# Seven products instead of eight in 30 weight blocks of a float32 encoder layer on one core

## The chip, the cores and the metric

The kernel runs on one core of one Trainium2 chip. The metric is the device time of one execution in microseconds; the median of three runs is compared. One more execution was profiled, and all rows below are from it.

## The reference

One encoder layer over 256 tokens of width 2048, in float32:

```python
z = rmsnorm(x, mix_norm) @ w_in          # latents, conv inputs, memory queries, 3*2048 gates
y_mla  = mla_attention(...) @ w_o_mla    # 8 heads
y_conv = (cb * dwconv3(cc * cv)) @ w_out_conv
y_mem  = memory_attention(...) @ w_o_mem # 4 heads, 256 memory tokens
gates  = sigmoid(g + gate_bias)          # (256, 3, 2048)
x = x + (gates[0]*y_mla + gates[1]*y_conv + gates[2]*y_mem) @ w_o
u = dwconv3(rmsnorm(x, ffn_norm) @ w_up) # 2*5632 columns
a, b = split(u)
x = x + (silu(a) * b) @ w_down           # 5632 -> 2048
return rmsnorm(x, final_norm)
```

## The kernel before

Every float32 matrix product is made of float32r halves: a value is its rounded part `hi` plus the rest `lo`, and a product is hi·hi + hi·lo + lo·hi, three matmuls. Weights come from HBM in blocks of 1 MB (128 partitions x 2048 floats) into the pool `raws` (3 buffers), issued on SP's queue (`load`, L130). For each block ScalarE copies `raw` to `hi` (L144) and VectorE subtracts, `lo = raw - hi` (L145); `his` has 3 buffers, `los` 2. Tokens and other activations are kept as pairs side by side in one tile: 256 columns of hi, 256 of lo, in a pool `slots` of 54 tiles. PSUM has two pools, `mmps` (5 banks) and `atps` (3 banks).

The program is written in order, stage by stage, without loops on the chip; a scheduler orders the instructions of each engine by priority and hands out buffers, so an engine's queue can differ a little from the source's order. Within an engine the order is then fixed, and each instruction waits for what it needs.

Stages: latents of the tokens, whose `xs` hold x times the norm's gain but not the token's own factor `rsb` (1/rms); the keys of the memory tokens, during which `token_factor` (L341) gets `rs`, `rsb`, and `rs2b` = rsb squared; the values of the memory tokens (`values`, L385, blocks of 24 matmuls); attention heads, mixed with the short convolution (`gated_conv`, L582), which multiply by `rsb` or `rs2b` wherever a product of `xs` is used; the gates and branch projections (L699 to L717); the output projection; the up projection (`up`, L752, 2 groups of 22 chunks of 128 columns); after each group the down projection over that group's 22 chunks (L793 to L800); for the last 512 columns a version that keeps the last 10 pieces of weights and ends with the final norm.

The gates: for each of 4 column groups n and each of 3 branches, `project` (L657) forms the gate product of 16 token chunks (4 blocks) and then the branch's projection (8 chunks, 2 blocks). `project` takes 2 banks, one for each half of the tokens, and calls `multiply` (L671 to L676) for each chunk and half:

```python
nc.tensor.matmul(ps, xh, hi[:, s], start=first, stop=False)   # L674
nc.tensor.matmul(ps, xh, lo[:, s], start=False, stop=False)   # L675
nc.tensor.matmul(ps, xl, hi[:, s], start=False, stop=final)   # L676
```

The stationary operand is 128 tokens, the moving one 512 weight columns. A block of four chunks is thus 24 matmuls. The gate's bank is read by VectorE (L708: times rs, plus bias), sigmoid follows on ScalarE (L711), then L715 and L717 on VectorE multiply the branch and add. `turned` (L678) transposes the merged columns, 8 transposes and 4 splits for each n, called from inside the next projection (`flush`).

Of the kernel before, what the change touches and what calls it, by code (L numbers as in the profile page):

```python
# [19 lines left out]
P = 128  # L20
D = 2048
# [44 lines left out]
KEPT = 10  # L66
STEPS = "r - k0 v0 - q0 0 1 2 3 k1 v1 q1 4 5 - 6 - 7 -"
# [9 lines left out]
def tile_kernel(ctx: ExitStack, tc: tile.TileContext, a, out):  # L77
# [5 lines left out]
    los = ctx.enter_context(tc.tile_pool(name="los", bufs=2))  # L83
# [26 lines left out]
    x0 = slots.tile([P, 2 * T], F32, tag="raw", name="xr", bufs=4)  # L110
# [148 lines left out]
    class Tokens:  # L259
# [6 lines left out]
        def load(self, n):  # L266

            i = len(self.raw)
            t = self.raw[-1][0] if i % 2 else slots.tile([P, 2 * T], F32, tag="raw", name="xr", bufs=4)
# [71 lines left out]
    def token_factor():  # L341
# [11 lines left out]
        rs2b = const.tile([P, T], F32, name="rs2b")  # L353
        nc.vector.tensor_tensor(rs2b, rsb, rsb, op=ALU.mult)
        yield rs, rsb, rs2, rs2b
# [27 lines left out]
    rs, rsb, rs2, rs2b = next(own)  # L383
# [167 lines left out]
    for i in range(8):  # L551
        qx.append(scaled(total(mm(*wblock(), 0, xs)), rsb, f"qx{i}", XD**-0.5))
        if i == 0:
# [8 lines left out]
            nc.vector.tensor_tensor(half(kr, 0), ps[:, 0:T], rsb, op=ALU.mult)  # L562
# [19 lines left out]
    def gated_conv():  # L582
        for i in range(8):
# [6 lines left out]
            nc.vector.tensor_tensor(v, v, rs2b, op=ALU.mult)  # L590
# [3 lines left out]
            t = temp("t")  # L594
            nc.vector.tensor_tensor(t, total(mm(*wblock(), 0, xs)), rsb, op=ALU.mult)
            nc.vector.tensor_tensor(u, u, t, op=ALU.mult)
# [95 lines left out]
    mg = [slot(f"mg{i}", F32R) for i in range(KC)]  # L692
# [6 lines left out]
    for n in range(NW):  # L699
        ms_ = [slot(f"m{h}") for h in range(2)]  # L700
        for br, (w, src) in enumerate((("woa", oa), ("woc", yc), ("wom", om))):
            bias = wide("bias")
            nc.scalar.dma_start(bias, a["gb"][:, br * D + n * 512 : br * D + (n + 1) * 512])
            gp = project(a["wg"], br * NW + n, xs, flush)
            gs = []
            for h in range(2):
                g = ms_[h] if br == 0 else wide("g")
                nc.vector.scalar_tensor_tensor(  # L708
                    g, gp[h], rs[:, h : h + 1], bias, op0=ALU.mult, op1=ALU.add
                )  # L710
                nc.scalar.activation(g, g, AF.Sigmoid)  # L711
                gs.append(g)
            bp = project(a[w], n, src)
            for h in range(2):
                nc.vector.tensor_tensor(gs[h], bp[h], gs[h], op=ALU.mult)  # L715
                if br:
                    nc.vector.tensor_tensor(ms_[h], ms_[h], gs[h], op=ALU.add)  # L717
        pending.append(lambda ms_=ms_, n=n: turned(ms_, mg[4 * n : 4 * n + 4]))
# [31 lines left out]
    rfb = []  # L750

    def up(c):  # L752
# [25 lines left out]
        s = half(us, 0)  # L778
        nc.scalar.activation(s, half(vs, 0), AF.Silu)
        nc.vector.tensor_tensor(s, s, half(vs, 1), op=ALU.mult)  # L780
        f = slot(f"f{c}", F32R)
        split(f, s)
        return f
# [3 lines left out]
    for g in range(NG):  # L787
# [5 lines left out]
        for n in range(NW - last):  # L793
            ps = project(a["wdn"], g * NW + n, fs)
# [35 lines left out]
    src = a["wdn"][(NG - 1) * NW + n]  # L830
# [48 lines left out]

def _colmajor(v):  # L880

    return np.asarray(v).reshape(-1, P).T


def _layout(x, mem, positions, mix_norm, w_in, q_norm, w_uq, kv_norm, w_ukv, w_o_mla, conv_w,
# [11 lines left out]
    for i in range(8):  # L897
# [28 lines left out]
        "wg": _groups(w_in[0][:, o_g:]),  # L926
# [7 lines left out]
        "wdn": _groups(w_down[0], NG),  # L934
# [22 lines left out]
```

## Time and profile before

| | us |
|---|---|
| median of 3 runs (1629.28 to 1630.43) | 1630.28 |
| the profiled execution | 1630.0 |
| its span, first to last instruction | 1628.2 |
| TensorE busy with matmuls | 1612.4 |
| VectorE busy | 1061.1 |
| ScalarE busy | 797.7 |

The profiled execution is 0.28 below the median, and 1.8 of it lie outside the span. A matmul's duration in the rows includes its way through the array; what a stream of them costs is the distance between their starts. The granted clock is that of TensorE, as a share of its 2.4 GHz.

### The profile page before, as it was taken

To read this page: it belongs to the slowest core of one execution; us is meant where nothing else is said; L and a number is where in the kernel's file an instruction comes from. 1 tells how busy PE (TensorE), PEld (TensorE's weight loads), DVE (VectorE), ACT (ScalarE), POOL (GpSimd) and SP (SyncE) were. 2 spreads that over 40 slices of the span, in tenths; PEclk is the share of its full clock that TensorE was granted. 3 is DMA by queue.
4 is the path that set the end of the run, shared out by engine and by line. 5 is a ranking of instruction groups with operands and counts; after the bars stand their busy time and mean duration, and the time that the engine had idled before them with its cause. 6 is when DMAs were issued, how large, how long until landed. Compare 5 with 4: busy or idle time off the path is not lost.

```text
span 1628.2 us, 20547 instructions
## 1 busy us (share of the span) xinstructions
PE 1612.4 (99%) x8322; PEld 1382.8 (85%) x8322; DVE 1061.1 (65%) x1291; ACT 797.7 (49%) x955; POOL 12.6 (1%) x23
## 2 busy tenths in 40 slices
PE   9999999999999999999999999999999999999997
PEld 8888898888888888888788888888888888888886
DVE  6866779776455554555545877777445777777444
ACT  7754556554434343443444655555333555555433
POOL 0000000000000000000000000000000000000000
PEclk9999999999999999999999999999999999999999
DMA  8655445445565565656555455555555555555553
GB/s 314 227 219 191 161 164 197 155 169 181 184 210 194 196 212 185 215 201 205 189 207 194 181 183 196 190 183 193 179 205 197 183 196 191 183 193 197 204 194 116
DMA packets 52142, 314.77 MB, mean 193 GB/s; under 512 B 6096, under 2 KB 7504, under 8 KB 16592
## 3 DMA queue, kind: packets, MB, share of 16 engines
q1 hardware_dynamic: 47520, 306.73, 53.1%
q10 hardware_dynamic: 3888, 6.20, 1.2%
q8 instruction: 65, 1.06, 0.3%
q0 software_dynamic: 640, 0.52, 0.1%
q14 instruction: 29, 0.24, 0.0%
HBM read 310.16 MB, written 2.10 MB: 192 GB/s over the span
## 4 chain that ended last, share of the span: by engine, by line
PE 96%; DVE 1%; ACT 1%; DMA 1%; issue 1%; ACTq 0%; POOLq 0%; POOL 0%; DVEq 0%
PE ps L172 27%; PE ps L174 16%; PE ps L675 15%; PE ps L676 15%; PE ps L674 14%; PE ps L176 2%; PE ps L398 1%; PE ps L399 1%; PE ps L397 1%; PE pss L463 1%; PE ps L185 1%; DVE lo L145 1%; PE ps L189 0%; PE ps L685 0%; PE pst L487 0%
## 5 line engine op out<-in xcount | busy, mean ns | idle before, releaser
L145 DVE TENSOR_TENSOR lo<-raw,hi 128x2048 fp32r<-128x2048 f32 (+2 forms) x297 | 644.5, 2172 | 355.9 <-PE ps L675 190.3
L144 ACT ACTIVATE hi<-raw 128x2048 fp32r<-128x2048 f32 (+2 forms) x297 | 539.7, 1820 | 429.8 <-PE ps L676 388.7
L172 PE MATMUL ps<-h,hi 128*128 128x512 f32 x1845 | 447.0, 392 | 0.2 <-ACT kn L205 0.2
L172 PEld LDWEIGHTS ps<-h,hi 128*128 128x128 f32 x1845 | 344.7, 188 | 68.8 <-ACT kn L205 0.4
L174 PEld LDWEIGHTS ps<-h,lo 128*128 128x128 f32 x1968 | 252.8, 191 | 9.6 <-DVE lo L145 0.2
L174 PE MATMUL ps<-h,lo 128*128 128x256 f32 x1968 | 257.2, 283 | 0.0
L675 PE MATMUL ps<-lo,h 128*128 128x512 f32 x384 | 149.9, 390 | 0.0
L676 PE MATMUL ps<-hi,h 128*128 128x512 f32 x384 | 149.6, 390 | 0.0
L674 PE MATMUL ps<-hi,h 128*128 128x512 f32 x384 | 142.7, 390 | 0.0
L676 PE MATMUL ps<-hi,f 128*128 128x512 f32 x332 | 129.3, 389 | 0.0
L675 PE MATMUL ps<-lo,f 128*128 128x512 f32 x332 | 129.3, 389 | 0.0
L674 PE MATMUL ps<-hi,f 128*128 128x512 f32 x332 | 123.5, 389 | 0.0
L196 ACT ACTIVATE hl<-ps 128x256 f32<-128x256 f32 x149 | 57.0, 383 | 90.1 <-PE ps L176 77.8
L676 PEld LDWEIGHTS ps<-hi,h 128*128 128x128 f32 x384 | 72.1, 188 | 14.9
L674 PEld LDWEIGHTS ps<-hi,h 128*128 128x128 f32 x384 | 72.1, 188 | 14.8
L675 PEld LDWEIGHTS ps<-lo,h 128*128 128x128 f32 x384 | 72.1, 188 | 14.8
L571 ACT ACTIVATE v<-u,taps 128x256 f32<-128x256 f32 x88 | 44.8, 509 | 72.3 <-DVE u L776 72.3
L572 DVE SCALAR_TENSOR_TENSOR v<-u,taps,v 128x255 f32<-128x255 f32 x88 | 42.6, 484 | 48.8 <-ACT v L571 48.8
L675 PEld LDWEIGHTS ps<-lo,f 128*128 128x128 f32 x332 | 62.3, 188 | 13.0
L674 PEld LDWEIGHTS ps<-hi,f 128*128 128x128 f32 x332 | 62.4, 188 | 12.9
L676 PEld LDWEIGHTS ps<-hi,f 128*128 128x128 f32 x332 | 62.3, 188 | 12.8
L198 DVE TENSOR_TENSOR t<-ps,hl 128x256 f32<-128x256 f32 x149 | 62.1, 418 | 2.6 <-ACT hl L196 2.4
(263 smaller groups left out, 1714.0 us busy)
## 6 DMA issues: line engine op xcount, KB each, us to landing
raw<-in_wup SPq DMA_DIRECT2D x88, 1024.0 KB, 4.8
raw<-in_wg SPq DMA_DIRECT2D x48, 1024.0 KB, 4.8
raw<-in_wdn SPq DMA_DIRECT2D x40, 1024.0 KB, 4.8
raw<-in_win SPq DMA_DIRECT2D x35, 1024.0 KB, 4.8
raw<-in_wo SPq DMA_DIRECT2D x16, 1024.0 KB, 4.9
raw<-in_wmk SPq DMA_DIRECT2D x8, 1024.0 KB, 4.8
raw<-in_wmv SPq DMA_DIRECT2D x8, 1024.0 KB, 4.8
raw<-in_woa SPq DMA_DIRECT2D x8, 1024.0 KB, 5.0
```

The lines of the kernel that those rows point to most:

```text
L144: nc.scalar.activation(hi[:, s], raw[:, s], AF.Copy)
L145: nc.vector.tensor_tensor(lo[:, s], raw[:, s], f32(hi[:, s]), op=ALU.subtract)
L172: nc.tensor.matmul(ps, hi[:, ks[k]], xs[k], start=first and k == 0, stop=False)
L174: nc.tensor.matmul(ps[:, 0:T], lo[:, ks[k]], xs[k][:, 0:T], start=False, stop=False)
L176: nc.tensor.matmul(ps, hi[:, ks[k]], xs[k], start=False, stop=True)
L196: nc.scalar.activation(hl, ps[:, T:], AF.Copy)
L198: nc.vector.tensor_tensor(t, ps[:, 0:T], hl, op=ALU.add)
L571: nc.scalar.activation(dst, x, AF.Copy, scale=col(w, wn + wi))
L572: nc.vector.scalar_tensor_tensor(dst[:, 1:T], x[:, 0 : T - 1], col(w, wi), dst[:, 1:T], op0=ALU.mult, op1=ALU.add)
L674: nc.tensor.matmul(ps, xh, hi[:, s], start=first, stop=False)
L675: nc.tensor.matmul(ps, xh, lo[:, s], start=False, stop=False)
L676: nc.tensor.matmul(ps, xl, hi[:, s], start=False, stop=final)
```

## The change

Two chunks of input (a pair p, two token chunks x1 and x2 of 128 features) by two column groups of 512 and two halves of the tokens are a 2x2 by 2x2 product of submatrices. A plain block does its 8 products. A fast block does 7 (Winograd's form of Strassen's scheme): sums of the weight pieces are made in place in `raw` after the first pieces are split, and split again into a second pair of hi/lo buffers; sums of token pieces are made once and kept. Results stand in eight banks: q1, q6, q7, q5, q2 in `mmps` (in this order), q3, q4, d in `atps`. At the end VectorE combines them.

Fast blocks: pairs 1, 3, 5 of 8 in each of 6 gate products (18 blocks), pairs 1, 3, 5, 7 of 11 in three down products (12 blocks). The down projection's last 1024 columns of the second group stay as they were. The gates go branch by branch (2, 1, 0), two column groups at a time: one gate product of 8 pair blocks, then two projections of 2 blocks each. The tokens are normed early: the 8 pairs are loaded again (8 DMAs on SP's queue), multiplied by gain and `rsb` and split anew into `xs`, while the memory values are formed; the later multiplications by `rsb`, `rs2b` and `rs` fall away. `los` has 3 buffers instead of 2, paid by the 4 tiles that held raw tokens, which now share the pool of `wide`.

```diff
+GATES = (1, 3, 5)
+FAST = (1, 3, 5, 7)
-    los = ctx.enter_context(tc.tile_pool(name="los", bufs=2))
+    los = ctx.enter_context(tc.tile_pool(name="los", bufs=3))
-    x0 = slots.tile([P, 2 * T], F32, tag="raw", name="xr", bufs=4)
+    x0 = wide("xr")
...
+    def normed(p):
+        t = wide("xn")
+        nc.sync.dma_start(t, a["xT"][:, 2 * p * T : 2 * (p + 1) * T])
+        for j in range(2):
+            h = half(t, j)
+            nc.vector.scalar_tensor_tensor(
+                h, h, col("mix", 2 * p + j), rsb, op0=ALU.mult, op1=ALU.mult
+            )
+            split(xs[2 * p + j], h)
     for n in range(2):
+        for p in range(4 * n, 4 * n + 4):
+            normed(p)
         vx.append(values(a["wmv"], n, 4, ms, "vx"))
...
-            nc.vector.tensor_tensor(v, v, rs2b, op=ALU.mult)
...
+    def token_sums(t):
+        a11, a21, a12, a22 = (t[:, i * P : (i + 1) * P] for i in range(4))
+        w = wide("sums")
+        s1, s2, s3, s4 = (w[:, i * P : (i + 1) * P] for i in range(4))
+        nc.vector.tensor_tensor(s1, a21, a22, op=ALU.subtract)
+        nc.vector.tensor_tensor(s3, a21, a11, op=ALU.subtract)
+        nc.vector.tensor_tensor(s2, a11, s1, op=ALU.subtract)
+        nc.vector.tensor_tensor(s4, a12, s2, op=ALU.subtract)
+        sh, sl = slot("sh", F32R), slot("sl", F32R)
+        nc.scalar.activation(sh, w, AF.Copy)
+        nc.vector.tensor_tensor(sl, w, f32(sh), op=ALU.subtract)
+        return sh, sl
+    class Two:
+        def __init__(self, src, xs, sums):
...
+            self.q = {name: psum() for name in ("q1", "q6", "q7", "q5", "q2")}
+            self.q.update({name: psum(atps, "at") for name in ("q3", "q4", "d")})
+        def add(self, name, xh, xl, hi, lo, piece):
+            s = slice(piece * 512, (piece + 1) * 512)
+            for x, w in ((xh, hi), (xh, lo), (xl, hi)):
+                nc.tensor.matmul(self.q[name], x, w[:, s], ...)
+        def plain(self, p):
+            hi, lo = block(self.src[:, p * WB : (p + 1) * WB])
+            for j, x in enumerate(self.xs[2 * p : 2 * p + 2]):
+                for h in range(2):
+                    for g in range(2):
+                        piece = ((0, 1), (3, 2))[j][g]
+                        self.add((("q2", "q3"), ("q4", "d"))[h][g], *self.part(x, h), hi, lo, piece)
+        def fast(self, p):
+            raw = next(load(self.src[:, p * WB : (p + 1) * WB]))
...
+            hi, lo = two(slice(0, 512), slice(1024, 2048))
+            nc.vector.tensor_tensor(raw[:, 0:1024], raw[:, 0:1024], raw[:, 512:1536], op=ALU.add)
+            nc.vector.tensor_tensor(b[2], b[0], b[2], op=ALU.add)
+            nc.vector.tensor_tensor(b[3], b[2], b[3], op=ALU.add)
+            hi2, lo2 = two(slice(0, 1024), slice(1024, 2048))
...
+            self.add("q1", *self.part(x1, 0), hi, lo, 0)
+            self.add("q3", *sums(4), hi, lo, 2)
+            self.add("q2", *self.part(x2_, 0), hi, lo, 3)
+            self.add("q5", *sums(1), hi2, lo2, 0)
+            self.add("q7", *sums(3), hi2, lo2, 1)
+            self.add("q6", *sums(2), hi2, lo2, 2)
+            self.add("q4", *self.part(x2_, 1), hi2, lo2, 3)
...
+    def gated(q, g, b1, b2):
+        (g11, g12), (g21, g22) = g
+        nc.scalar.activation(g11, q["q1"], AF.Copy)
+        to(g22, q["q6"], g11, ALU.subtract)
+        to(g12, g22, b2)
+        to(g12, g12, q["q5"])
+        to(g21, b1, g22, ALU.subtract)
+        to(g21, g21, q["q7"], ALU.subtract)
+        to(g22, g12, q["q7"])
+        to(g11, g11, b1)
+        for x, name in ((g11, "q2"), (g12, "q3"), (g21, "q4"), (g22, "d")):
+            to(x, x, q[name])
+            nc.scalar.activation(x, x, AF.Sigmoid)
+    for br, w, src in ((2, "wom", om), (1, "woc", yc), (0, "woa", oa)):
+        for jp in range(2):
...
+            q = Two(a["wg"][br * 2 + jp], xs, hsums).run()
+            gated(q, g, *bias)
+            for i in range(2):
+                bp = project(a[w], 2 * jp + i, src, flush)
...
-        for n in range(NW - last):
-            ps = project(a["wdn"], g * NW + n, fs)
+        for n in range(0, 2 if last else NW, 2):
+            q = Two(a["wd2"][g * NW // 2 + n // 2], fs, sums).run()
+            added(q, [[x2[h][n + i] for i in range(2)] for h in range(2)])
...
+        for n in range(2, NW - 1 if last else 2):
+            ps = project(a["wdn"], n - 2, fs)
```

(`two` splits the named pieces of `raw` into a fresh hi and a fresh lo buffer, ScalarE and VectorE; `added` is for the down projection what `gated` is for the gates: one copy and 12 additions into the residual; `token_sums` runs for 3 pairs before the gates and for 8 pairs in the up projection.)

How VectorE's queue changes in the gates. Before, between two gate products (`lo` is a block's rest, `ps` a bank):

```order
L145 TENSOR_TENSOR lo_4389<-raw_4386,hi_4388 128x2048 [waits DVE_49,DMAHW1_49,PE_49,Activation_49]
L708 SCALAR_TENSOR_TENSOR g_4378<-ps_4256,xr_1119,bias_4254 128x512 [waits DMAHW2_49,PE_49]
L145 TENSOR_TENSOR lo_4419<-raw_4416,hi_4418 128x2048 [waits DVE_49,DMAHW2_49,PE_49,Activation_49]
L708 SCALAR_TENSOR_TENSOR g_4381<-ps_4257,xr_1119,bias_4254 128x512 [waits PE_49]
L145 TENSOR_TENSOR lo_4457<-raw_4454,hi_4456 128x2048 [waits DVE_49,DMAHW3_49,PE_49,Activation_49]
L715 TENSOR_TENSOR g_4378<-ps_4384,g_4378 128x512 [waits PE_49,Activation_49]
```

Now, a plain block (lo_4677), a fast block (first pair of buffers lo_4707, second lo_4716), a plain block, and the first reading of a bank:

```order
L147 TENSOR_TENSOR lo_4677<-raw_4674,hi_4676 128x2048 [waits DMAHW3_49,Activation_49]
L767 TENSOR_TENSOR lo_4707<-raw_4704,hi_4706 128x512 [waits DMAHW4_49,Activation_49]
L767 TENSOR_TENSOR lo_4707<-raw_4704,hi_4706 128x1024 [waits Activation_49]
L771 TENSOR_TENSOR raw_4704<-raw_4704 128x1024 [waits DVE_49]
L772 TENSOR_TENSOR raw_4704<-raw_4704 128x512 [waits DVE_49]
L773 TENSOR_TENSOR raw_4704<-raw_4704 128x512 [waits DVE_49]
L767 TENSOR_TENSOR lo_4716<-raw_4704,hi_4715 128x1024 [waits Activation_49] x2
L147 TENSOR_TENSOR lo_4745<-raw_4742,hi_4744 128x2048 [waits DMAHW5_49,Activation_49]
L833 TENSOR_TENSOR g_4805<-ps_4531,g_4802 128x512 [waits PE_49,Activation_49]
L147 TENSOR_TENSOR lo_4775<-raw_4772,hi_4774 128x2048 [waits DMAHW6_49,Activation_49]
```

One subtraction of 2048 columns for a block has become five pieces of subtraction and three additions for a fast block, between plain ones; and the bank ps_4531 (q6) is read two plain blocks before the product's end.

TensorE's queue at the start of the last gate product (branch 0, second half). Here ps_6264 to ps_6271 are q1, q6, q7, q5, q2, q3, q4, d; hi_6274 is block 0 (plain), hi_6304 and hi_6313 the two buffers of block 1 (fast), hi_6342 block 2 (plain), hi_6372 the first of block 3. Before, where one product follows another:

```order
L674 MATMUL ps_5056<-hi_5150,h12_309 128x512 [waits Activation_49]
L674 MATMUL ps_5057<-hi_5150,h12_309 128x512
L674 MATMUL ps_5184<-hi_5188,om0_0_1735 128x512 [waits Activation_49]
L674 MATMUL ps_5185<-hi_5188,om0_0_1735 128x512
L675 MATMUL ps_5056<-lo_5151,h12_309 128x512 [waits DVE_49]
L676 MATMUL ps_5056<-hi_5150,h12_309 128x512
L675 MATMUL ps_5057<-lo_5151,h12_309 128x512
```

Now ("..." leaves out matmuls of the same blocks):

```order
L741 MATMUL ps_6268<-hi_6274,h0_141 128x512 [waits Activation_49]
...
L741 MATMUL ps_6264<-hi_6304,h2_173 128x512 [waits Activation_49]
...
L741 MATMUL ps_6270<-hi_6274,h0_141 128x512 [waits DVE_49,PE_49]
...
L741 MATMUL ps_6267<-hi_6313,sh_4074 128x512 [waits Activation_49]
...
L741 MATMUL ps_6265<-hi_6313,sh_4074 128x512 [waits DVE_49,Activation_49]
...
L741 MATMUL ps_6271<-hi_6274,h0_141 128x512 [waits DVE_49,PE_49]
...
L741 MATMUL ps_6271<-hi_6274,h1_160 128x512
...
L741 MATMUL ps_6268<-hi_6342,h4_199 128x512 [waits Activation_49]
...
L741 MATMUL ps_6264<-hi_6372,h6_227 128x512 [waits Activation_49]
L741 MATMUL ps_6268<-lo_6343,h4_199 128x512 [waits DVE_49]
```

Block 0's products into d (ps_6271) stand behind most of block 1's, the last of them as the 41st matmul, since d's bank waits for VectorE; and after four matmuls of block 2's `hi` comes one of block 3's before block 2's `lo` is used.

## Rows read from the trace of the kernel before

**Rows 1.** The first lines of the page: the span, and of each engine the busy time, its share of the span and the instructions (PE is matmuls, PEld weight loads).

```profile
span 1628.2 us, 20547 instructions
...
PE 1612.4 (99%) x8322; PEld 1382.8 (85%) x8322; DVE 1061.1 (65%) x1291; ACT 797.7 (49%) x955; POOL 12.6 (1%) x23
```

**Rows 2.** Who made TensorE's matmuls wait, over the whole span: microseconds in total, times, longest. There are no other rows.

```profile
PE ps L675 <- DVE lo L145: 1.9, 2, 1.2
PE ps L182 <- ACT h L208: 1.8, 1, 1.8
PE ps L290 <- POOL ident masks.py:199: 1.5, 1, 1.5
PE ps L172 <- DVE m L209: 1.3, 1, 1.3
PE ps L172 <- ACT kn L205: 0.2, 1, 0.2
```

**Rows 3.** TensorE's instructions in order of time in the gate and projection stage: start, duration, engine, line, tile. From the first row to the last there are 12 steps, every matmul a row.

```profile
759.76 0.39 PE L676 MATMUL ps<-hi,yc 128*128 128x512 f32 x1
...
762.48 0.39 PE L676 MATMUL ps<-hi,yc 128*128 128x512 f32 x1
```

**Rows 4.** Busy time of the engines in stretches (microseconds from the span's start; the columns are TensorE, weight loads, VectorE, ScalarE, GpSimd, then the granted clock, the DMA share and GB/s): the two blocks of values of the memory tokens, the attention stage, the gates, the up projection, the down projection.

```profile
100.00:147.00 47.00, 47.00 (x219) 39.18 (x219) 24.93 (x28) 18.22 (x17) 1.38 (x2) 1.00 0.52 186
300.00:350.00 50.00, 50.00 (x296) 44.25 (x295) 41.28 (x70) 30.03 (x52) 0.00 (x0) 1.00 0.46 168
700.00:800.00 100.00, 100.00 (x447) 82.86 (x446) 53.58 (x40) 39.34 (x28) 0.00 (x0) 1.00 0.59 199
1000.00:1100.00 100.00, 100.00 (x576) 88.42 (x575) 79.06 (x108) 56.10 (x72) 0.00 (x0) 1.00 0.52 189
1150.00:1250.00 100.00, 100.00 (x443) 82.81 (x442) 44.93 (x26) 35.00 (x20) 0.00 (x0) 1.00 0.56 196
```

**Rows 5.** Groups of instructions by line and shape, for the gate product (stationary tokens h) and the down projection (f): count, busy time, mean ns. A matmul here has 128 rows and 512 columns.

```profile
L675 PE MATMUL ps<-lo,h 128*128 128x512 f32 x384 | 149.9, 390 | 0.0
L675 PE MATMUL ps<-lo,f 128*128 128x512 f32 x332 | 129.3, 389 | 0.0
```

**Rows 6.** Groups on VectorE by shape: count, busy time, mean ns of one, idle time before them.

```profile
L145 DVE TENSOR_TENSOR lo<-raw,hi 128x2048 fp32r<-128x2048 f32 x272 | 623.1, 2291 | 323.8 <-PE ps L675 168.3 <-issue 67.4 <-PE ps L174 64.9
L145 DVE TENSOR_TENSOR lo<-raw,hi 128x1024 fp32r<-128x1024 f32 x9 | 10.9, 1225 | 22.0 <-PE ps L675 22.0
L145 DVE TENSOR_TENSOR lo<-raw,hi 128x512 fp32r<-128x512 f32 x16 | 10.5, 689 | 10.1 <-ACT hi L144 10.0
L717 DVE TENSOR_TENSOR m<-m,g 128x512 f32<-128x512 f32 x16 | 10.3, 683 | 0.0
L715 DVE TENSOR_TENSOR g<-ps,g 128x512 f32<-128x512 f32 x16 | 11.0, 688 | 25.3 <-PE ps L676 25.3
L708 DVE SCALAR_TENSOR_TENSOR g<-ps,xr,bias 128x512 f32<-128x512 f32 x16 | 12.0, 748 | 24.7 <-PE ps L676 24.7
L206 DVE TENSOR_TENSOR mg<-ps,mg 128x256 fp32r<-128x256 f32 x16 | 6.4, 423 | 4.0 <-ACT mg L205 3.6
L209 DVE SCALAR_TENSOR_TENSOR h<-xr,cols,h 128x256 fp32r<-128x256 f32 x16 | 7.0, 480 | 0.0
L252 DVE TENSOR_SCALAR dg<-ident,mr 128x128 f32<-128x128 f32 x2 | 0.5, 284 | 0.6 <-POOL mr L239 0.6
```

**Rows 7.** Groups on ScalarE by shape, same columns.

```profile
L144 ACT ACTIVATE hi<-raw 128x2048 fp32r<-128x2048 f32 x272 | 520.9, 1915 | 398.9 <-PE ps L676 364.0 <-PE ps L399 17.4 <-issue 6.5
L144 ACT ACTIVATE hi<-raw 128x1024 fp32r<-128x1024 f32 x9 | 9.4, 1058 | 24.7 <-PE ps L676 24.7
L144 ACT ACTIVATE hi<-raw 128x512 fp32r<-128x512 f32 x16 | 9.4, 624 | 6.1 <-DMA raw<-in_wkv 6.0
L711 ACT ACTIVATE g<-g 128x512 f32<-128x512 f32 x16 | 10.0, 624 | 4.2 <-DVE g L708 4.2
```

**Rows 8.** All engines in order of time around the end of one block: TensorE leaves a block (762.48), starts the next (762.71), and VectorE and ScalarE start to write the buffer that came free.

```profile
762.71 0.39 PE L675 MATMUL ps<-lo,h 128*128 128x512 f32 x1
762.90 2.28 DVE L145 TENSOR_TENSOR lo<-raw,hi 128x2048 fp32r<-128x2048 f32 x1
762.96 1.92 ACT L144 ACTIVATE hi<-raw 128x2048 fp32r<-128x2048 f32 x1 [3.97 <-PE ps L676]
```

**Rows 9.** DMA issues by tile: queue, count, KB each, median microseconds from issue to landing.

```profile
raw<-in_wg SPq DMA_DIRECT2D x48, 1024.0 KB, 4.8
xr<-in_xT SPq DMA_DIRECT2D x6, 256.0 KB, 5.3
```

**Rows 10.** VectorE in order of time where a latent's factor is worked out, with the wait for GpSimd's power in brackets.

```profile
115.31 0.16 DVE L365 SCALAR_TENSOR_TENSOR kvf<-kvr,xr 128x2 f32<-128x2 f32 x1 [0.80 <-POOL kvr L239]
```

**Rows 11.** ScalarE's copies of weight blocks in the up projection, in order of time: start, duration. From the first row to the last there are 17 steps, each copy a row.

```profile
1001.48 1.91 ACT L144 ACTIVATE hi<-raw 128x2048 fp32r<-128x2048 f32 x1
...
1096.11 1.91 ACT L144 ACTIVATE hi<-raw 128x2048 fp32r<-128x2048 f32 x1
```

**Rows 12.** The chain that ended last, in order of time, in the output projection's stretch: start, duration, what.

```profile
811.60 2.30 DVE lo L145
823.70 2.30 DVE lo L145
```

More of the change, by code (lines that the diff above doesn't have):

```diff
@@ L352, in token_factor @@
         nc.vector.tensor_tensor(rs2, rs, rs, op=ALU.mult)
-        rs2b = const.tile([P, T], F32, name="rs2b")
-        nc.vector.tensor_tensor(rs2b, rsb, rsb, op=ALU.mult)
-        yield rs, rsb, rs2, rs2b
+        yield rs, rsb, rs2
     def latent_factor(sq, name, scale):
@@ L382, in tile_kernel @@
             next(own)
-    rs, rsb, rs2, rs2b = next(own)
+    rs, rsb, rs2 = next(own)
     def values(src, n, nblk, xs, name):
@@ L551, in tile_kernel @@
     for i in range(8):
-        qx.append(scaled(total(mm(*wblock(), 0, xs)), rsb, f"qx{i}", XD**-0.5))
+        qx.append(slot(f"qx{i}", F32R))
+        split(qx[i], total(mm(*wblock(), 0, xs)), XD**-0.5)
         if i == 0:
@@ new lines, in added, with plus @@
+    def added(q, c):
+        def plus(x, y, op=ALU.add):
+            nc.vector.tensor_tensor(x, x, y, op=op)
+        c1, u = wide("c1"), wide("u")
+        nc.scalar.activation(c1, q["q1"], AF.Copy)
+        plus(c[0][0], c1)
+        nc.vector.tensor_tensor(u, q["q6"], c1, op=ALU.subtract)
+        plus(c[1][0], u, ALU.subtract)
+        plus(c[1][0], q["q7"], ALU.subtract)
+        plus(u, q["q5"])
+        plus(c[0][1], u)
+        plus(c[1][1], u)
+        plus(c[1][1], q["q7"])
+        plus(c[0][0], q["q2"])
+        plus(c[0][1], q["q3"])
+        plus(c[1][0], q["q4"])
+        plus(c[1][1], q["d"])
@@ L693, in tile_kernel @@
+    mg = [None] * KC
     pending = []
@@ L697, in flush @@
             pending.pop(0)()
[L699 to L718, printed above, removed]
+    hsums = {}
@@ new lines, in tile_kernel, with to @@
+    for p in GATES:
+        t = wide("t")
+        for j in range(2):
+            x = f32(xs[2 * p + j])
+            nc.vector.tensor_tensor(half(t, j), x[:, 0:T], x[:, T:], op=ALU.add)
+        hsums[p] = token_sums(t)
+    def gated(q, g, b1, b2):
+        def to(x, y, z, op=ALU.add):
+            nc.vector.tensor_tensor(x, y, z, op=op)
+        (g11, g12), (g21, g22) = g
[10 more added lines that the diff above has]
+            nc.scalar.activation(x, x, AF.Sigmoid)
@@ L747, in tile_kernel @@
         )
-    rfb = []
+    rfb, pair, sums = [], [], {}
     def up(c):
@@ L778, in up @@
         s = half(us, 0)
+        p, j = c % GF // 2, c % 2
+        if p in FAST:
+            if j == 0:
+                pair.append(slot("pair"))
+            s = half(pair[-1], j)
         nc.scalar.activation(s, half(vs, 0), AF.Silu)
@@ L782, in up @@
         split(f, s)
+        if p in FAST and j == 1:
+            sums[p] = token_sums(pair.pop())
         return f
@@ L877, in _groups, with _quads @@
     return t.reshape(parts * (n // 512), P, -1)
+def _quads(w, parts=1):
+    k, n = w.shape
+    t = w.reshape(parts, k // (2 * P * parts), 2, P, n // 1024, 2, 512)
+    t = t.transpose(0, 4, 3, 1, 2, 5, 6).reshape(parts, n // 1024, P, -1, 4, 512)
+    t = t[:, :, :, :, [0, 1, 3, 2]]
+    return t.reshape(parts * (n // 1024), P, -1)
 def _colmajor(v):
```

72 lines of the change are left out of this document (63 added, 9 removed).

## The prediction

> **What bounds the kernel now.** I read the page's first lines, then who made TensorE wait, then the matmuls one by one, then the stretches. TensorE is busy 1612.4 of 1628.2 us [rows 1], and of the 15.8 that are left the list of waits holds 6.7 [rows 2]; the rest lies at the ends of the span. So there is next to no stall to win; time goes only if matmuls go. What one costs is read from starts, not durations: 12 steps take 762.48 - 759.76 = 2.72 us, 0.227 us each, though each row says 0.39 [rows 3]. A plain block of 24 matmuls is therefore 5.44 us. The clock is 1.00 of 2.4 GHz in all stretches shown, and VectorE, the next busiest, has 53.6 of 100 us in the gates, 44.9 in the down projection, 79.1 in the up projection, and 41.3 of 50 in the attention stage [rows 4].
>
> The Trainium skill (Perfetto Trace Analysis, section Identifying the Most-Contended Engine) says that matmul busy time is no good measure of TensorE's headroom and that the share of weight loads is. That share is 85% here [rows 1]; by this rule TensorE would not be at its limit and removing matmuls might bring nothing, 1630 us. The rows with starts decide: the matmuls follow each other without a gap.
>
> **What the change removes.** A fast block has 7 products of 3 matmuls instead of 8: 21 x 0.227 = 4.76 us instead of 5.44. There are 18 fast blocks in the gates and 12 in the down projection, all of 512 columns and of the shape whose groups are shown [rows 5]: 30 x 3 x 0.227 = **20.4 us** off TensorE. Nothing is added to TensorE.
>
> **What it adds, and what hides it.** On VectorE a plain block is one subtraction of 2.29 us. A fast block is 0.69 + 1.225 for its first two pieces, an addition over 1024 columns, two over 512, and 2 x 1.225 for the second buffer [rows 6]. The additions (in place, both inputs in SBUF) have no row of their own form over 1024 columns; the nearest is the in-place addition L717 at 0.683 for 512 columns and the 1024-wide subtraction at 1.225. I take 1.225 + 2 x 0.683; the lower bound is the same (nothing of that size is cheaper), the upper 0.748 for each 512, as L708 has it [rows 6], 0.4 us more. A fast block is then 6.96 us on VectorE, more than its 4.76 on TensorE. But fast blocks alternate with plain ones: a pair of blocks takes 10.20 us on TensorE, 9.25 (at most 9.65) on VectorE and 0.62 + 3 x 1.06 + 1.92 = 5.72 on ScalarE [rows 7]. The pair is covered if VectorE need not stand idle.
>
> Whether it must, I walk through with the buffers. A fast block takes two of the three hi/lo buffers, so each buffer comes free only when TensorE leaves the block before last; ScalarE then starts 0.25 us later (762.96 - 762.71) [rows 8]. Let F be the start of a fast block. The next plain block's copy runs from F+0.25 to 2.2, its subtraction to 4.5; needed at 4.76 plus the five matmuls that stand ahead of its `lo` (1.1). The next fast block's first buffer comes free after 9 matmuls, F+2.3; VectorE turns to it at 4.5 and has the pieces at 6.4, the three additions at 9.0, the second buffer's pieces at 10.3 and 11.5. TensorE starts that block at 10.2, wants the first of them at 12.2, the last at 13.6. So VectorE is ahead by 1 to 2 us at each place, and idle 0.9 us a pair. The weights are not late: a block lands 4.8 us after its issue [rows 9], and its buffer in `raws` (three of them) comes free about two blocks, 10 us, before it is wanted.
>
> The combining: `gated` is 11 VectorE instructions of 0.69, a copy and four sigmoids of 0.62 on ScalarE; the four readings L708 per two column groups go. Over one gate product with its two projections VectorE has 3 x 6.96 + 9 x 2.29 + 11 x 0.69 + 4 x 0.69 = 52 us (55 with the additions across branches), TensorE 3 x 4.76 + 9 x 5.44 = 63.2. Only the last four readings (q2, q3, q4, d) follow the product's end; q1, q5, q6, q7 are complete after pair 5 and read during the plain blocks behind it. So the projection finds q1's and q6's banks free and does not wait. Cost 0.
>
> Norming adds 16 x 0.48 + 16 x 0.42 = 14.4 us on VectorE [rows 6] in the values' stretch, which has 24.9 busy of 47 [rows 4]: it fits (39.3), if the tokens come in time; 5.3 us to landing [rows 9] against buffers free about 5 us before. Bounds 0 and 2 us; I take 0, since the one wait for GpSimd there is 0.8 us [rows 10] and a `lo` is a block ahead. `rs2b` and the 24 or so multiplications by `rsb` go, 0.42 each, off a VectorE that was not waited for: 0. The token sums in the up projection (8 x (4 x 0.28 + 0.69) = 14.5 us there): two chunks are four blocks of weights, 5.57 us each ((1096.11 - 1001.48) / 17, [rows 11]), 22.3 us on TensorE; VectorE has 79% of it, 17.6, plus 1.8: 19.4. Covered: 0.
>
> **Three places where it does not fit.** (a) The first gate product. The token sums for the gates and the last convolution stand in VectorE's queue between this product's pieces: from behind block 0's subtraction to block 5's last piece I count 53 instructions, 37.6 us by their rows. They can start about 6.5 us ahead of the product, when the third-last block is left, and so end 31 us after its start, while TensorE would want block 4 at 20.4 and block 5's last piece at 29. Piece by piece this makes waits of 0.4, 0.9, 0.7, 0.3 and 0.2: 2.5 us; between 0 (if the queue is drained earlier) and 6 (if none of it starts ahead). (b) The last gate product: the transposes of the merged columns hold banks of `atps`, and block 0's products into d come as late as the 41st matmul. Block 0's buffer is left at 9.3 instead of 5.44 us, the copy of block 2 ends at 11.4, 1.2 after TensorE wants it, the subtraction at 13.8, 1.2 after it is wanted: 2.4 us. (c) The second down product follows the first without a projection between: by the same reasoning (35 matmuls) the copy is in time and the subtraction 1.0 late. Sum 5.9 us.
>
> **What the third `los` buffer gives.** Twice VectorE's `lo` is on the path in the output projection, 1.9 us in all [rows 2, 12], because with two buffers a `lo` can be written only one block ahead. With three this goes: -1.9 (bounds 0 and -1.9).
>
> Small waits at 30 fast blocks, each with some four more hand-overs, have no row; the shortest wait in the list is 0.2 [rows 2], so 0 to 6 us; I take 1.0, since the walk leaves over 1 us at most of them.
>
> **Sum.** -20.4 + 5.9 - 1.9 + 1.0 = -15.4 us against the profiled execution's 1630.0: 1614.6; against the median, 0.28 higher, **1615 us**.
>
> **Rivals.**
>
> Nothing waits: the three places are absorbed by VectorE being ahead. For it: back-to-back rows on VectorE start a little before the one in front ends, so my sums are on the high side. -20.4 - 1.9: 1608. Chance 0.09.
>
> Every product loses what the three lose: 9 products x 2 us = 18, and little is left: 1629, no change that can be told. For it: VectorE's queue waits in order for the last bank readings at each product's end, with the next blocks' pieces behind them; against: the walk has these pieces a block ahead. Chance 0.08.
>
> The banks. All eight belong to one product, so at its end TensorE may have to wait for VectorE's four last readings, 0.25 + 4 x 0.69 = 3.0 us [rows 6]: 9 x 3.0 = 27, and 1630.3 - 20.4 + 27 + 3 = 1640, slower. It decides if the next product's first banks are those of q2, q3, q4 or d. The queue speaks against it, except at (b) and (c), where it puts other matmuls in between. Chance 0.05.
> The Trainium skill (Perfetto Trace Analysis, section Matmuls) says that independent groups should rotate through banks so that the reading of one overlaps the next group's matmuls, which speaks against eight banks for one product; by that rule this rival decides, and no run shown so far has such a product.
>
> VectorE becomes the bound. If the in-place additions over overlapping pieces cost double, a fast block is 9.55 us and a pair 11.84 against the 10.88 of two plain blocks before: 30 x 0.96 = 29 us slower, 1659. It decides from 10.88 a pair, that is additions at 1.6 times the price of L717. For it: no row shows inputs that overlap the output. Against: L717 is in place too and keeps the price of an ordinary one. Chance 0.04.
>
> That the matmuls do not go is ruled out by the built program's order: it has 5586 of 512 columns instead of 5676.
>
> **How the numbers follow.** Forecast 0.74; the rivals 0.09, 0.08, 0.05, 0.04. Two runs of this kernel can be told apart from about 0.2%, 3.3 us. Faster: 0.74 + 0.09 = 0.83; same 0.08; slower 0.09. The range: its lower end is the case with no wait, 1608; its upper end is the sum with (a) at 6, the norming at 2, small waits at 6 and no gain from `los`: -20.4 + 9.4 + 2 + 6 = -3.0, 1627, less a little since these will hardly all come together: 1626.
>
> **What would show it.** Right: 21 matmuls per fast block 0.227 apart; VectorE near 9.3 us per pair of blocks in the gates, its share there up from 54 to over 80%; TensorE's waits for `lo` or `hi` in the gates and the down projection below 8 us in all, most of them in the first and last gate products. Wrong: waits of about 1 us at every fast block (VectorE), at every product's start for a bank (the banks), or an addition over 1024 columns well above 1.23 us.

## The result and the profile after

| | before | changed |
|---|---|---|
| median, us | 1629.78 | 1620.13 |
| ratio, 95% interval | | 0.9942 (0.993 to 0.9954) |
| span of the profiled execution, us | 1628.2 | 1616.9 |

The change makes the kernel 9.4 us faster (0.9942 of 1629.78); 15.3 were forecast, 1615 us with a range of 1608 to 1626, which holds the result. In the profiled executions the spans differ by 11.3 us, and it is these that the traces explain. The page of the changed kernel begins so (compare [rows 1]):

```profile
span 1616.9 us, 20751 instructions
...
PE 1593.2 (99%) x8232; PEld 1368.4 (85%) x8232; DVE 1244.7 (77%) x1601; ACT 839.4 (52%) x1079; POOL 12.5 (1%) x23
```

8232 matmuls instead of 8322: the 90 are gone. VectorE has 310 more instructions and 184 us more work. Who made TensorE wait in the changed kernel, the whole list (compare [rows 2]):

```profile
PE ps L174 <- DVE t L200: 6.2, 1, 6.2
PE ps L174 <- DVE m L211: 4.8, 1, 4.8
PE ps L184 <- ACT h L210: 1.6, 1, 1.6
PE ps L292 <- POOL ident masks.py:199: 1.5, 1, 1.5
```

No row speaks of L741, the line of all products in pair blocks, nor of L685 to L687: the list knows of no wait in the gates and the down projection, and the 1.9 us for `lo` in the output projection are gone. Instead there are two single waits, in parts of the kernel that the change was thought to pass by: for a piece of the memory tokens (`m`) and for the reading of a bank (`t`).

To see which stage gains and which loses, take TensorE's first matmul of three stages: the values of the memory tokens, the gates, the up projection. Before:

```profile
100.66 0.47 PE L397 MATMUL ps<-hi,m 128*128 128x512 f32 x1
...
400.36 0.40 PE L674 MATMUL ps<-hi,h 128*128 128x512 f32 x1
...
888.29 0.39 PE L760 MATMUL ps<-h,hi 128*128 128x512 f32 x1
```

And in the changed kernel:

```profile
104.60 0.47 PE L397 MATMUL ps<-hi,m 128*128 128x512 f32 x1
...
411.66 0.40 PE L741 MATMUL ps<-hi,h 128*128 128x512 f32 x1
...
884.74 0.39 PE L914 MATMUL ps<-h,hi 128*128 128x512 f32 x1
```

Ahead of the gates the changed kernel loses 11.3 us (3.9 of them before the values). From the gates to the up projection it takes 473.1 us instead of 487.9, 14.85 less; 18 fast blocks at 0.68 are 12.3, the waits for `lo` 1.9, and 0.65 is left over. From there to the end it gains 7.75 (12 fast blocks: 8.2). So the counted gain came nearly in full, and a loss that no term of the sum had took half of it.

**The wait near 67 us.** SP's queue, the DMA issues in order of time: start, duration. Before:

```profile
57.07 2.29 SPq L271 DMA_DIRECT2D xr<-in_memT  x2
69.20 0.33 SPq L135 DMA_DIRECT2D raw<-in_xr  x1
```

In the changed kernel, with the matmuls that the wait delays behind them (TensorE's rows):

```profile
56.08 0.33 SPq L273 DMA_DIRECT2D xr<-in_memT  x1
58.58 0.33 SPq L137 DMA_DIRECT2D raw<-in_xr  x1
61.02 0.33 SPq L273 DMA_DIRECT2D xr<-in_memT  x1
```

```profile
66.78 0.58 PE L174 MATMUL ps<-m,hi 128*128 128x512 f32 x1 [4.84 <-DVE m L211]
67.16 3.41 PE L176 MATMUL ps<-m,lo 128*128 128x256 f32 x15
```

The 1 MB load of the residual now stands between the last two loads of memory tokens (256 KB each). The last of these is issued at 61.02 (before: 59.03) and split at 66.2; TensorE stands still for 4.84 us, before for 1.29 [rows 2]. The later issue is not all of it. The tokens have landed at 64.15, but ScalarE, which makes the first half of the split, has the residual's sum of squares (L348) ahead of them in its queue:

```profile
63.50 1.91 ACT L348 ACTIVATE raw<-raw 128x2048 f32<-128x2048 f32 x1 [0.60 <-DMA raw<-in_xr]
...
65.71 0.49 ACT L210 ACTIVATE m<-xr,cols 128x256 fp32r<-128x256 f32 x1
```

Before, ScalarE stood idle for the landing of the tokens and split them at once (61.79). The early load of the residual thus delays the tokens on two queues.

**The wait near 268 us.** TensorE in the attention stage of the changed kernel, then VectorE's queue in front of the reading that it waits for (the last row; L460 begins the rotary work of the second pair, L639 makes the low halves of the exchange):

```profile
261.88 0.39 PE L178 MATMUL ps<-h,hi 128*128 128x512 f32 x1
268.45 5.27 PE L174 MATMUL ps<-h,hi 128*128 128x512 f32 x15 [6.18 <-DVE t L200]
```

```profile
255.70 0.42 DVE L200 TENSOR_TENSOR t<-ps,hl 128x256 f32<-128x256 f32 x1
257.65 0.43 DVE L460 TENSOR_TENSOR qr<-qr,rot 128x256 f32<-128x256 f32 x1 [1.54 <-DMA sw<-qr]
...
259.67 2.28 DVE L147 TENSOR_TENSOR lo<-raw,hi 128x2048 fp32r<-128x2048 f32 x1
261.88 1.77 DVE L639 TENSOR_TENSOR ql<-qr,qr 64x256 fp32r<-64x256 f32 x4
...
265.69 2.28 DVE L147 TENSOR_TENSOR lo<-raw,hi 128x2048 fp32r<-128x2048 f32 x1
267.89 0.41 DVE L200 TENSOR_TENSOR t<-ps,hl 128x256 f32<-128x256 f32 x1
```

The bank was complete at about 246 us. Its reading stands behind a wait for a DMA (the rotary halves), two block subtractions and sixteen small instructions, 12 us in all; the program before has the rotary work of the second pair two readings earlier in the queue. The 15 matmuls behind the wait take 5.27 us; the same group at 281.31 takes 3.58.

### The profile page after: what moved, and what is told of

It is laid out like the page before. It is cut to its first block, busy times and chain, and to the rows that moved or that the text cites. A ratio compares the mean times of both kernels' runs of the same rounds, so it can differ in the third digit from the quotient of the medians.

```text
span 1616.9 us, 20751 instructions
## 1 busy us (share of the span) xinstructions
PE 1593.2 (99%) x8232; PEld 1368.4 (85%) x8232; DVE 1244.7 (77%) x1601; ACT 839.4 (52%) x1079; POOL 12.5 (1%) x23
## 4 chain that ended last, share of the span: by engine, by line
PE 97%; DVE 1%; issue 1%; DMA 1%; ACT 0%; POOLq 0%; POOL 0%; ACTq 0%; DVEq 0%
PE ps L174 28%; PE ps L741 26%; PE ps L176 16%; PE ps L686 6%; PE ps L685 6%; PE ps L687 6%; PE ps L178 2%; PE ps L397 1%; PE ps L399 1%; PE ps L398 1%; PE pss L476 1%; PE ps L187 1%; PE ps L191 0%; PE ps L696 0%; PE pst L500 0%
## 5 line engine op out<-in xcount | busy, mean ns | idle before, releaser
L147 DVE TENSOR_TENSOR lo<-raw,hi 128x2048 fp32r<-128x2048 f32 (+2 forms) x264 | 575.2, 2181 | 243.7 <-ACT hi L146 243.0
L146 ACT ACTIVATE hi<-raw 128x2048 fp32r<-128x2048 f32 (+2 forms) x264 | 481.4, 1826 | 209.9 <-PE ps L687 72.0
L741 PE MATMUL ps<-hi,h 128*128 128x512 f32 x588 | 188.1, 389 | 0.0
L766 ACT ACTIVATE hi<-raw 128x512 fp32r<-128x512 f32 (+1 forms) x120 | 110.3, 948 | 131.2 <-DVE raw L771 72.7
L767 DVE TENSOR_TENSOR lo<-raw,hi 128x512 fp32r<-128x512 f32 (+1 forms) x120 | 128.0, 1086 | 10.3 <-ACT hi L766 10.1
L741 PE MATMUL ps<-hi,f 128*128 128x512 f32 x408 | 129.8, 389 | 0.0
L741 PEld LDWEIGHTS ps<-hi,h 128*128 128x128 f32 x588 | 110.4, 188 | 22.9
L741 PE MATMUL ps<-lo,h 128*128 128x512 f32 x294 | 114.6, 390 | 0.0
L741 PEld LDWEIGHTS ps<-hi,f 128*128 128x128 f32 x408 | 76.6, 188 | 15.8
L741 PE MATMUL ps<-lo,f 128*128 128x512 f32 x204 | 79.4, 389 | 0.0
L741 PEld LDWEIGHTS ps<-lo,h 128*128 128x128 f32 x294 | 55.2, 188 | 11.9 <-DVE lo L147 0.6
L685 PE MATMUL ps<-hi,mg 128*128 128x512 f32 x128 | 49.7, 392 | 0.0
L686 PE MATMUL ps<-lo,mg 128*128 128x512 f32 x128 | 49.7, 389 | 0.0
L687 PE MATMUL ps<-hi,mg 128*128 128x512 f32 x128 | 49.5, 389 | 0.0
L741 PE MATMUL ps<-lo,sh 128*128 128x512 f32 x120 | 46.7, 389 | 0.0
```

Source lines behind the costliest of these rows:

```text
L146: nc.scalar.activation(hi[:, s], raw[:, s], AF.Copy)
L147: nc.vector.tensor_tensor(lo[:, s], raw[:, s], f32(hi[:, s]), op=ALU.subtract)
L741: nc.tensor.matmul(self.q[name], x, w[:, s], start=name not in self.begun, stop=self.left[name] == 0,)
L766: nc.scalar.activation(hi[:, s], raw[:, s], AF.Copy)
L767: nc.vector.tensor_tensor(lo[:, s], raw[:, s], f32(hi[:, s]), op=ALU.subtract)
```

## The experiments

Theory A: the third `lo` buffer, together with the norming, changes the order in which loads and VectorE's instructions are queued ahead of the gates, and that order makes the two waits. Theory B: the norming's own work (VectorE, loads) makes them. Theory C: the fast blocks cost more than they show.

**e1, all blocks plain.**

```
-GATES = (1, 3, 5)
-FAST = (1, 3, 5, 7)
+GATES = ()
+FAST = ()
...
(gated and added read q2, q3, q4, d alone, and a product takes only these four banks)
```

> The changed kernel with every block plain (no fast block in the gates or the down projection; the token sums and the additions that combine go with them); its order up to the first gate product is the changed kernel's. If the 30 fast blocks give what was counted and nothing is lost in the gates and the down projection, this is 20.4 us slower than the changed kernel, 1640.5 us, and the two stalls ahead of the gates (4.8 us at 67 us, 6.2 us at 268 us) stand in it too. If hand-overs or VectorE eat part of the gain there, the difference is smaller: 14 us or less for the 5.9 of waits that were forecast, 1634.

Measured: 1640.04 us, 1.006 (1.0043 to 1.0076) of the kernel before and 19.9 above the changed kernel. TensorE's waits:

```profile
PE ps L174 <- DVE t L200: 6.3, 1, 6.3
PE ps L174 <- DVE m L211: 4.6, 1, 4.6
...
```

No row of its list speaks of the gates. The fast blocks give 19.9 of the 20.4, and both waits stand without a single fast block. Theory C falls. From the gates to the up projection e1 takes 485.0 us against the changed kernel's 473.1: 11.9 of the 12.3 counted there. Everything else in the change together (norming, order of the gates, third buffer) makes the kernel 10.6 us slower.

**e2, two `lo` buffers.**

```
-    los = ctx.enter_context(tc.tile_pool(name="los", bufs=3))
+    los = ctx.enter_context(tc.tile_pool(name="los", bufs=2))
```

> The changed kernel with two lo buffers instead of three. Theory A (the third buffer changes the order in which loads and VectorE's instructions are queued ahead of the gates, and this makes the two stalls): both stalls are gone, 12 us less before the gates; within the gates and the down projection a fast block's second lo buffer can only be written when the plain block in front of it is left, so TensorE waits 0.5 to 1.2 us for it at each of the 30, 15 to 36 us; 1623 to 1644 in all. Theory B (the stalls come from the norming's own work, 16 x 0.9 us on VectorE and 8 transfers): the stalls stay, 1635 to 1656.

Measured: 1677.93 us, 58 above the changed kernel. Both waits ahead of the gates are gone (0.9 and 0.5 are left of them), and the gates and the down projection wait everywhere:

```profile
PE ps L741 <- ACT hi L766: 17.5, 16, 1.1
PE ps L741 <- DVE lo L147: 15.9, 22, 1.0
PE ps L741 <- DVE lo L767: 10.8, 16, 0.7
```

So the third buffer is needed where the fast blocks are: 70 us, reckoned from a kernel without the two waits, about twice the 15 to 36 that were expected. Ahead of the gates it does harm. Theory B falls, as far as the norming alone is meant: the norming is all in this kernel, and so is the sharing of the `wide` pool by the raw tokens.

**e3, the kernel before with three `lo` buffers.**

```
-    los = ctx.enter_context(tc.tile_pool(name="los", bufs=2))
+    los = ctx.enter_context(tc.tile_pool(name="los", bufs=3))
-    x0 = slots.tile([P, 2 * T], F32, tag="raw", name="xr", bufs=4)
+    x0 = wide("xr")
...
(the same in Tokens.load)
```

> The kernel before with three lo buffers (the raw tokens share the pool of the wide tiles, as in the change), nothing else. Theory A: the load of the residual moves ahead of the last memory tokens on SP's queue, so the stall near 67 us appears, 3 to 5 us with the slower clock behind it; the two waits for lo in the output projection, 1.9 us, go: 1631 to 1633. Theory B: no new stall, only the 1.9 us go: 1628.

Measured: 1634.60 us, 1.0033 (1.002 to 1.0046) of the kernel before. TensorE's waits, and SP's queue:

```profile
PE ps L172 <- DVE m L209: 4.9, 1, 4.9
PE ps L397 <- ACT hi L144: 2.0, 1, 2.0
...
PE ps L172 <- DVE t L198: 0.9, 1, 0.9
```

```profile
56.61 0.33 SPq L271 DMA_DIRECT2D xr<-in_memT  x1
59.12 0.33 SPq L135 DMA_DIRECT2D raw<-in_xr  x1
61.82 0.33 SPq L271 DMA_DIRECT2D xr<-in_memT  x1
```

The third buffer, with the raw tokens in the `wide` pool as in the change, puts the residual's load between the memory tokens and makes the kernel slower, without norming and without fast blocks. The run changes two things, the buffer and the pool of the raw tokens, and it takes both: with the shared pool and two buffers (e2) the two waits are gone, and with three buffers and one more wide tile (e6, below) the tokens go ahead of the residual. The gates start at 408.63 instead of 400.36: 8.3 us lost ahead of them. From there to the up projection it takes 485.0 us instead of 487.9, so in the gates and the output projection the third buffer gives 2.9 us, 1.0 more than the two waits in the list. The loss ahead of the gates was larger than expected, and so is the time (1631 to 1633 were expected). The wait near 268 us is not here in its size (smaller ones are), so for that one the norming's other queue has a part.

**e4, the third buffer for fast blocks alone.**

```
+    lox = ctx.enter_context(tc.tile_pool(name="lox", bufs=1))
...
+            hi2, lo2 = two(lox, slice(0, 1024), slice(1024, 2048))
```

(and `los` back to 2)

> The changed kernel with two lo buffers in the common pool and the third in a pool of its own that only a fast block's second pair of pieces uses. Theory A: the order ahead of the gates is as with two buffers, both stalls are gone (-12 us), the gates keep what they need, the 1.9 us in the output projection come back: 1610 us. Theory B: the stalls stay, 1622 us.

Measured: 1614.50 us, 0.9908 (0.9893 to 0.9922). Both waits are gone, the gates start at 399.37, but from there to the up projection it takes 481.95 us, 8.9 more than the changed kernel:

```profile
PE ps L742 <- DVE lo L148: 3.1, 8, 0.8
PE ps L687 <- DVE lo L148: 1.9, 2, 1.2
```

A buffer that only one kind of block may use is worth less than one in the common pool; 1.9 of the 8.9 are the two waits in the output projection, as before the change. (The list counts idle time only: a matmul that starts up to 0.16 us late, behind one of 0.39 that began 0.227 before, is in no row.)

**e5, two buffers up to the gates, three in turn from there.**

```
+    def low_tile():
+        if turn:
+            turn.append(1)
+        pool = lox if turn and len(turn) % 3 == 0 else los
+        return pool.tile([P, WB], F32R, tag="lo", name="lo")
...
+    turn.append(1)
     hsums = {}
```

> The changed kernel with two lo buffers up to the gates and three in turn from the gates on (two from the common pool, then one of its own, and so on). Theory A (the third buffer reorders the queues ahead of the gates, and that alone makes the two stalls): the stage ahead of the gates as in e4 (12.3 us less than the changed kernel), the gates as in the changed kernel (8.9 less than e4, whose waits for lo go), together 1606 to 1608 us. If the stalls went in e4 for another reason, or the gates need the one common pool: 1612 to 1616.

Measured: 1611.35 us, 0.9889 (0.9872 to 0.9905): 8.8 below the changed kernel. The gates start at 400.05, as in the kernel before (400.36), with the norming in place: it costs nothing there. From the gates to the up projection: 476.87, 3.8 more than the changed kernel; of 2.4 us of listed waits, 2.2 are in the first gate product, the longest two of them:

```profile
418.60 0.73 PE L749 MATMUL ps<-hi,sh 128*128 128x512 f32 x2 [0.69 <-ACT hi L774]
422.74 0.50 PE L749 MATMUL ps<-lo,h 128*128 128x512 f32 x1 [0.67 <-DVE lo L155]
```

These are waits that the prediction put there (place (a)). That they don't show in the changed kernel because TensorE, held up by 11 us before, comes later to work that VectorE has done meanwhile is argued and not shown: e5 also hands out its third buffer in a fixed turn, and no run has three common buffers and an early start of the gates.

**e6, a fifth buffer for the wide tiles.**

```
-.get(name, ("w", 4))
+.get(name, ("w", 5))
...
(bufs=5 in wide, too)
```

> The changed kernel with a fifth buffer for the wide tiles, in which the raw memory tokens are loaded; three lo buffers as in the change. The last two loads of memory tokens then stand ahead of the load of the residual on SP's queue again. Theory A: the stall near 67 us goes (4.9 us), the one near 268 us stays unless VectorE's order moves too: 1615 us. If the stall near 67 us comes from VectorE's work and not from the load: 1620.

Measured: 1620.11 us, no change. The memory tokens are loaded ahead of the residual and the wait for `m` is gone, but another is in its place:

```profile
PE pss L255 <- DVE dg L254: 3.8, 2, 2.9
```

TensorE now waits near 90 us for VectorE's `dg`, the tile that spreads a factor over the columns; in VectorE's queue it stands behind a block subtraction (89.68 to 91.97 us). The values of the memory tokens start at 106.90, even later than in the changed kernel. By its time alone the run would speak for the second case of the expectation; its trace shows the first, with the gain lost again in the same stage. What put `dg` behind that block was not followed further.

**e7, the keys ahead of the rotary queries.**

```
-STEPS = "r - k0 v0 - q0 0 1 2 3 k1 v1 q1 4 5 - 6 - 7 -"
+STEPS = "- k0 r v0 - q0 0 1 2 3 k1 v1 q1 4 5 - 6 - 7 -"
```

> The changed kernel with the first keys projected ahead of the rotary queries (two steps of the attention stage change places), so that the readings of the keys' banks stand ahead of the two waits for the exchange of the rotary halves in VectorE's queue. Theory A: the stall near 268 us (6.2 us and slower matmuls behind it, 7.4 in all) goes or shrinks, the one near 67 us stays: 1613 us; a smaller gain if another reading is late in its place. If the stall came from the norming itself: 1620.

Measured: 1615.73 us, 0.9915 (0.99 to 0.993), 4.4 below the changed kernel. The wait for `t` shrinks from 6.2 to 2.4 us, the one for `m` (4.6) stays. The place of the rotary work in VectorE's queue sets most of this wait (3.8 of 6.2 us).

**e8, four fast pairs in the gates** (e5 with `GATES = (1, 3, 5, 7)`).

> As e5, with a fourth fast pair in each gate product (1, 3, 5, 7 instead of 1, 3, 5): 18 matmuls fewer, 4.1 us. If alternating blocks stay covered at the product's end too: 1602 to 1604 us. Against it: the last block is then a fast one, all eight banks are read after it, and a gate product with its two projections has 56.6 us of work on VectorE for 62.6 on TensorE: if that waits, each product loses 2 to 3 us, 1615 to 1622.

Measured: 1612.38 us, 1.0 above e5, where 4.1 less were counted. The list has four waits in the first gate product, one in the third and four in the last, 5.0 us in all, for `hi` and `lo` of fast and of plain blocks.

The second and the fourth product have no wait, and each takes 62.58 us with its projections (from 467.51 to 530.09 and from 593.82 to 656.40) against 63.24 in e5: there the fourth fast pair gives 0.66 of the 0.68 counted. So VectorE covers four fast pairs of eight in the middle of the stage; the gain is lost in the first, the third and above all the last product. Whether a later first fast block, as in e9, would save it was not run.

**e9, fast pairs 2, 4, 6** (e5 with `GATES = (2, 4, 6)`).

> As e5, with the fast pairs of the gates at 2, 4, 6 instead of 1, 3, 5: the same 18 fast blocks, but in the first gate product VectorE gets one more plain block (10.9 us instead of 5.4 of TensorE's time) before the first fast block is wanted. If the first product's waits in e5 (2.2 us listed, 3 with the slower start of each) come from the token sums that stand among its pieces on VectorE's queue, they go: 1608 us. If they come from the fast blocks themselves, they only move: 1611.

Measured: 1607.13 us, 0.9866 (0.985 to 0.9883), the fastest here, 13 below the changed kernel. In the whole trace three rows are left, none of them behind 63 us:

```profile
PE ps L192 <- ACT h L218: 1.7, 1, 1.7
PE ps L300 <- POOL ident masks.py:199: 1.5, 1, 1.5
PE ps L182 <- DVE m L219: 0.9, 1, 0.9
```

One more plain block ahead of the first fast one is enough; this fits the case in which the token sums made the waits. From the gates to the up projection 473.19 us, the changed kernel's 473.1 without its late start. That is 22.0 us below the kernel before (1629.14 in these runs), close to what was counted: 20.4 for the matmuls and 1.9 for the waits for `lo`.

**e10, fast pairs 1, 2, 3** (e5 with `GATES = (1, 2, 3)`).

> As e5, with the fast pairs of the gates at 1, 2, 3, one behind the other; the number of matmuls and VectorE's work are the same. If the cover rests on the alternation (a fast block is some 6.5 us on VectorE against 4.76 on TensorE, and takes two of three lo buffers), TensorE waits at the second and third, 2 to 4 us a product, 12 to 24 in all: 1623 to 1635. If only the sum over a product counts (52 us on VectorE, 63 on TensorE): 1611.

Measured: 1623.07 us, 11.7 above e5. From the gates to the up projection 488.8 us, 12.0 more. The same work in another order: behind three fast blocks each product waits for the next plain block's `lo`, and the first and last for `hi`; 6.9 us are listed; the rest are late starts that the list doesn't count and a stretch at the lower clock in the first product (last section). The cover rests on the alternation.

## Why the prediction was right in direction and 5 us short

**What bounds the kernel, and what a matmul costs.** Right. 0.227 us a matmul from the starts [rows 3] gave 20.4; e1 measures 19.9. The stages give 22.6 (14.85 + 7.75), which leaves 19.7 without the 2.9 that the third buffer gives in e3. The Trainium skill (Perfetto Trace Analysis, section Identifying the Most-Contended Engine) would have had it that TensorE was not at its limit at a weight-load share of 85%; the share is 85% after as well, and the time fell with the matmuls, so here the rows with starts decided.

**What a fast block costs VectorE.** Right. The groups of the changed kernel on VectorE by shape:

```profile
L767 DVE TENSOR_TENSOR lo<-raw,hi 128x1024 fp32r<-128x1024 f32 x90 | 109.2, 1220 | 1.1 <-ACT hi L766 1.1
L771 DVE TENSOR_TENSOR raw<-raw 128x1024 f32<-128x1024 f32 x30 | 36.6, 1220 | 0.2
L772 DVE TENSOR_TENSOR raw<-raw 128x512 f32<-128x512 f32 x30 | 20.7, 690 | 0.8
```

The overlapping in-place addition over 1024 columns takes 1.22 us, as taken from the subtraction [rows 6], so a fast block is 6.95 us (6.96 forecast), and the rival in which VectorE is the bound falls. Over the gates VectorE has 82% (54 in [rows 4]):

```profile
420.00:770.00 350.00, 350.00 (x1549) 289.56 (x1548) 287.31 (x274) 173.43 (x151) 0.00 (x0) 1.00 0.58 211
```

**The banks.** Right: no wait of TensorE for a bank at a product's end is listed in any trace here. The Trainium skill (Perfetto Trace Analysis, section Matmuls) asks for banks in turn; with all eight in one product the queue put a projection or other matmuls in between, and the rule did not decide.

**The three places.** (a), 2.5 us: the mechanism is there, 2.2 us of listed waits in e5, gone when the first fast block comes later (e9), and not in the changed kernel (hidden, if the argument under e5 holds). (b), 2.4, and (c), 1.0: wrong, no wait is listed. The step that failed in (b) is "block 0's buffer is left at 9.3 instead of 5.44 us, the copy of block 2 ends at 11.4". TensorE and ScalarE in the last gate product, which begins at 729.10 (block 1's last use of its first `hi`, block 0's last product into d, the copy of block 2):

```profile
735.00 0.39 PE L741 MATMUL ps<-hi,h 128*128 128x512 f32 x1
...
738.17 0.39 PE L741 MATMUL ps<-hi,h 128*128 128x512 f32 x1
```

```profile
735.47 1.92 ACT L146 ACTIVATE hi<-raw 128x2048 fp32r<-128x2048 f32 x1 [3.83 <-issue]
```

The copy begins 0.24 us after block 1's first buffer is left and 2.9 before block 0 is done: the copy of block 2 did not wait for block 0's buffer, as I had walked it (buffers in turn), but was given the one that came free first. e4 fits this: a third buffer that cannot be handed about so costs 8.9 us. Of the 1.0 of small waits none is listed either; no run shows why.

The sums on VectorE's side are also a little high: I took TensorE by starts but VectorE by durations. Its rows in the gates:

```profile
505.73 0.68 DVE L833 TENSOR_TENSOR g<-ps,g 128x512 f32<-128x512 f32 x1
506.33 2.28 DVE L147 TENSOR_TENSOR lo<-raw,hi 128x2048 fp32r<-128x2048 f32 x1
508.52 0.68 DVE L833 TENSOR_TENSOR g<-g,bias 128x512 f32<-128x512 f32 x1
```

Instructions that don't need each other's results start 0.08 us before the one in front ends (0.60 for 0.68, 2.19 for 2.28). Over the 53 instructions of place (a) that is up to 4 us by my estimate. It is not what made (a) vanish: block 5's last piece, reckoned 31 us behind the product's start, ends at 29.0 in the changed kernel, which starts the product late, but at 32.2 in e5, which starts it on time.

**The norming**, "I take 0": right for its own work (e5: the gates start at 400.05).

**"What the third `los` buffer gives ... bounds 0 and -1.9": the step that failed.** The 1.9 came, and 1.0 more in the same stage (e3), but I let the lower bound of its gain be nothing, though no row excluded a loss. The buffer lets the scheduler place blocks earlier (the weight block issued at 55.96 us before is issued at 51.41), all other queues are built around that and around the shared pool of wide tiles, and they end up with the residual's load in front of the memory tokens and the rotary work in front of a bank's reading: 8.3 us ahead of the gates in e3, 11.3 with the norming. The order that the program was built with was at hand, and I had read it only in the gates.

So two errors met: 6.9 us of waits that did not come, and 11.3 us that had no term, together 4.4 against the 4.1 by which the profiled execution missed the sum. The forecast mechanism is right; the time came out above the forecast by a loss in a stage that was not looked at. That the result lies in the range is in part luck: the range's upper end was made of other terms, none of them for this loss, and the waits that did not come left room for it.

## What to carry to other kernels

A buffer added to a pool that the whole program uses is a change to the whole program: compare the order of every queue in every stage, not only where the buffer is wanted, and consider a bound on the side of loss. Work moved onto a second engine is covered here by alternation and by a lead at its start, and a sum over a stage does not show it; the first block of the kind needs time ahead of it. When a gain arrives short, take the starts of stages on the bounding engine in both traces first: they say in which stage to look.

## What was not expected of the hardware

Behind the two waits TensorE's matmuls were slower for a while. In the stretch around the longer one the granted clock is 0.85 of 2.4 GHz, that is, part of it at the lower level; TensorE had stood still for 6.2 us just before:

```profile
262.00:285.00 23.00, 16.82 (x84) 14.24 (x83) 17.30 (x32) 11.77 (x20) 2.04 (x4) 0.85 0.45 149
```

The 15 matmuls of 512 columns behind it take 5.27 us against 3.58 for the same group at full clock, and the 15 of 256 columns behind the wait near 67 us take 3.41 where 16 take 2.08 at full clock (the granted clock is 0.83 from 65 to 75 us). Each of the two waits costs about 1.5 us more than the list shows. The waits of up to 1.2 us between 400 and 900 us of e4 leave the clock at 1.00. In the first gate product of e10 TensorE stood still for 1.50 us up to 414.77 and for 0.45 up to 415.72, and a stretch soon after has part of its time at the lower level:

```profile
417.00:421.00 4.00, 4.00 (x12) 3.08 (x12) 4.00 (x5) 1.39 (x3) 0.00 (x0) 0.57 0.46 128
```
